# Start offsets of attention and out-projection tiles, the place of the meta keys, and the issue point of a local head's loads

## The chip, the core and the metric

One core of a Trainium2 chip. A core has TensorE (PE, which takes weight loads and matmuls in separate queues, PEld and PE), VectorE (DVE), ScalarE (ACT), GpSimd (POOL) and SyncE (SP, which here issues the DMAs); they run side by side and wait for each other by semaphores. The metric is the device time of one execution in microseconds. Three executions of the kernel before took 2195.36, 2196.57 and 2197.52 us: the median is 2196.57.

## The reference

One layer of an encoder with two groups of heads, run on a prompt of 1024 tokens and a sample of 256, each with 16 meta tokens ahead. All data are float32, the model width is 2048, a head has 128 columns.

```
u = rms_norm(h, norm_w) @ w_in                     # 2048 -> 6656
qa, ka, va, za, qb, kb, vb, zb = split(u)          # a: 8 heads, 2 of keys;  b: 8 heads
ya = global_gqa(rope(norm(qa)), rope(norm(ka)), va) * silu(za)   # every query sees every key
yb = neighbourhood_attention(norm(qb), norm(kb), vb, rpb) * silu(zb)
                                                   # 8 x 16 window on a grid 64 wide, plus the meta keys
y  = concat([ya, yb]) @ w_out                      # 2048 -> 2048
return h + y
```

Heads 0 to 7 are called global here, 8 to 15 local. Only real tokens are returned; the meta tokens take part as 16 more keys of each head.

## The kernel before

A product of two float32 matrices is made in three matmuls: each operand is split into a high part in the type fp32r and the rest (`split`, L59: a CAST on ACT at L61, a subtraction on DVE at L62), and hi×hi, hi×lo and lo×hi are summed in PSUM. A tile is a piece of SBUF that a pool hands out; a pool places its tiles one behind the other, at multiples of 32 bytes in each partition unless the call names `align_bytes`. `ALIGN` is 128 (L35); the tiles of x and of the output weights (`wm`, L917) already name it. A framework draws up the semaphores, and its planner sets the order in which each engine gets its instructions: work is emitted in the order of the program text, weight strips with a higher priority than what stands before them (L185), and the planner fills TensorE's waits with strips.

Three stages follow each other.

*First half* (`chunk1`, L565). 512 columns of tokens: the sample's 256, the prompt's first 240 and 16 of meta tokens. Each strip of 128 columns of w_in is loaded, split and multiplied by all 16 tiles of x (`strips`, L176; the matmuls L210 to L212). Keys, queries, values and gates of the prompt's part go to DRAM: `kd`, `qd` for global heads (two halves, hi and lo), `kfd`, `qfd` for local ones, `vn`, `vmd`, `zd`. The meta keys, the last 16 columns of the strip, are stored ahead of the 240 in `kd` and `kfd`, in a store of their own. The sample's attention is computed here.

*Second half* (`chunk2`, L688). The prompt's other 784 columns, in blocks of 512 and 272. For a global head, `k_first`, `v_tiles`, `q_strip` and `z_strip` make k, v, q and z whole (1024 columns; k has 1040, with the meta keys at columns 0 to 15), and `attend` (L321) runs on four blocks of 256 queries: scores with 8 tiles of keys (L332 to L334), their maxima and sums, exponentials, and probabilities times values (L372 to L374), where `ph` and `pl` are the split probabilities. The 16 meta keys are handled together with their low parts as an operand of 7 × 16 = 112 columns, `km` (`copy_km`, L501; `meta_scores`, L272 and L273), and one matmul with `vm` (L375).

The strips of the local heads (k, q, z, v: 32 in all, `late`) are projected as filling between these blocks and after them; their outputs go to DRAM (`k2d`, `q2d`, `zd`, `vn` by way of transposes L491 and stores L494, L499). The local heads' attention comes from a generator, `local_blocks` (L821): for each head it loads k (`k_load`, L778: `kfd` and `k2d`), v in four windows (`v_windows`), the bias table, q (`q_load`: `qfd` and `q2d`, then a split) and z, and yields after each of four blocks (`attend_strip`, L416: scores L438 on unsplit data, `qfull` and `kfull`, meta scores L272/L273, value products L467 and L470). 28 of its 32 blocks are drawn between the late strips, so that the loads of head h+1 are emitted when the first block of that head is asked for, behind a strip. The pools of k, v, table, q, z and qf have one buffer each, so a load waits until the preceding head has read its tile for the last time.

*Out-projection* (`outproj`, L974). Seven products of half matrices take the place of eight (Winograd's form), in the order 1, 2, 5, 6, 7, 3, 4: five token tiles × two column halves × 24 matmuls each, 70 × 24 = 1680 matmuls (`products`, L935 to L937). The operand loaded into TensorE is `yo` (128 tokens × 8 heads, high and low, from `yd` in DRAM by L884, split at L61/L62), the operand that streams through is `wm` (512 columns, from `ww`). The last local head's four blocks are drawn one after each of the first four products.

All DMAs of this part are issued on SP's queue, in one order; an issue that waits holds all behind it.

Of the kernel before, what the change touches and what calls it, by code (L numbers as in the profile page):

```python
# [20 lines left out]
P = 128  # L21
# [5 lines left out]
NS = 256  # L27
# [27 lines left out]
class Kern:  # L55
# [265 lines left out]
    def attend(self, q, zs, keys, meta, vals, vmeta, ydst):  # L321
# [43 lines left out]
        for j in range(nt):  # L365
            p, i = divmod(j, 2)
            if i == 0:
                ph = self.ph.tile([P, 2, QB], F32R, tag="ph", name="ph")
                pl = self.ph.tile([P, 2, QB], F32R, tag="pl", name="pl")
                self.split(ph[:], pl[:], S[p][:])  # L370
# [45 lines left out]
    def attend_strip(self, q, qf, zs, k, meta, vals, vmeta, tab, w, ydst):  # L416
# [17 lines left out]
        for t in (0, 3, 1, 2):  # L434
            a, e = groups[t]
            dst = part(pa, pb, t)
            o = NMETA + 256 * t + 32 * WIN0[w]
# [63 lines left out]
    def copy_km(self, k):  # L501

        km = self.k.tile([P, 7, NMETA], F32R, tag="km", name="km")
        for i, c, n in ((0, 0, 4), (1, 4, 3)):
            self.nc.scalar.copy(km[:, c:c + n], k[:, i, :].bitcast(F32).unsqueeze(1).to_broadcast([P, n, NMETA]))
        return km[:].rearrange("p c m -> p (c m)")
# [58 lines left out]
    def chunk1(self):  # L565
# [12 lines left out]
        def kb_strip(s, g, wc):  # L578
            kf = self.k.tile([P, T1], F32, tag="k1", name="kcf")

            def evac(ps):
                self.qk_evac(ps[0], 0, T1, wc, None, [], kf[:])
                nc.sync.dma_start(self.kfd[g][:, :NMETA], kf[:, PM:])
                nc.sync.dma_start(self.kfd[g][:, NMETA:], kf[:, NS:PM])
                km = self.k.tile([P, 3, NMETA], F32, tag="km", name="kmf")
                nc.scalar.copy(km[:], kf[:, PM:].unsqueeze(1).to_broadcast([P, 3, NMETA]))
                return kf, km[:].rearrange("p c m -> p (c m)")
# [13 lines left out]
        def k_strip(s, g, wc, rope):  # L601
            kt_ = self.k.tile([P, 2, T1], F32R, tag="k1", name="kc1")

            def evac(ps):
                self.qk_evac(ps[0], 0, T1, wc, (ct, st) if rope else None, [(0, T1, kt_[:, 0, :], kt_[:, 1, :])])
                nc.sync.dma_start(self.kd[g][:, :, :NMETA], kt_[:, :, PM:].bitcast(F32))
                nc.sync.dma_start(self.kd[g][:, :, NMETA:], kt_[:, :, NS:PM].bitcast(F32))
# [80 lines left out]
    def chunk2(self):  # L688
# [10 lines left out]
        K0 = NMETA + C1P  # L699

        def k_first(g):
            k = self.k.tile([P, 2, NMETA + NP], F32R, tag="k1", name="kf")
            nc.sync.dma_start(k[:, :, :K0].bitcast(F32), self.kd[g][:])
            return k, self.copy_km(k[:, :, :NMETA])

        def k_strip(s, g, wc, rope):
            k, km = k_first(g)

            def evac(ps):
                for p, (o, n) in zip(ps, BL):  # L710
                    rp = (ct[:, o:o + n], st[:, o:o + n]) if rope else None
                    self.qk_evac(p, o, n, wc, rp, [(0, n, k[:, 0, K0 + o:K0 + o + n], k[:, 1, K0 + o:K0 + o + n])])
# [10 lines left out]
        def v_tiles(g):  # L723

            h, l = (self.v.tile([P, 8, P], F32R, tag=f"v{i}", name="va") for i in range(2))
# [5 lines left out]
        def v_windows(h):  # L731

            v = []
            for i in range(2):
                t = self.v.tile([P, 8, P], F32, tag=f"v{i}", name="vw")
# [6 lines left out]
        def q_strip(s, h, wc, rope):  # L742
            q = self.q.tile([P, 2, NP], F32R, tag="q", name="q")
# [34 lines left out]
        def k_load(g):  # L778
            k = self.k.tile([P, NMETA + NP], F32, tag="k1", name="kfull")
            nc.sync.dma_start(k[:, :K0], self.kfd[g][:])  # L780
            nc.sync.dma_start(k[:, K0:], self.k2d[g][:])
# [430 lines left out]
```

## Time and profile before

| | |
|---|---|
| median of three executions | 2196.57 us |
| the profiled execution's own time | 2197.35 us |
| its span, first to last instruction | 2195.5 us |
| mean granted TensorE clock | 0.996 |
| busy: PE, PEld, DVE, ACT, POOL | 2166.0, 1879.9, 1650.8, 1125.7, 519.8 us |
| DMA moved | 383.82 MB, mean 175 GB/s |

Times in a profile count from the span's start; 1.85 us of the execution lie outside the span. Matmuls are pipelined: the duration of one (for a projection with 512 columns about 390 ns) is longer than its distance to the next, so a stream's pace is read from the starts. A line such as `L937 PE MATMUL pq<-wm,yo 128*128 128x512 f32 x560 | 223.2, 399 | 0.5 <-DVE yo L62 0.5` gives the line, engine, operation, output and inputs, the loaded operand's shape, the streamed one's, the count, then the busy time in us and the mean of one in ns, then the idle time of the engine just before them and what ended it. PE's busy share in 40 slices is 97% or more in nearly all; the exceptions lie at the start and at 1770 to 1790 us, where the second half ends.

```profile
PE   8999999999999999999999999999999979999999
PEclk9999999999999999999999999999999989999999
```

### The profile page before, as it was taken

To read this page: it belongs to the slowest core of one execution; us is meant where nothing else is said; L and a number is where in the kernel's file an instruction comes from. 1 tells how busy PE (TensorE), PEld (TensorE's weight loads), DVE (VectorE), ACT (ScalarE), POOL (GpSimd) and SP (SyncE) were. 2 spreads that over 40 slices of the span, in tenths; PEclk is the share of its full clock that TensorE was granted. 3 is DMA by queue.
4 is the path that set the end of the run, shared out by engine and by line. 5 is a ranking of instruction groups with operands and counts; after the bars stand their busy time and mean duration, and the time that the engine had idled before them with its cause. 6 is when DMAs were issued, how large, how long until landed. Compare 5 with 4: busy or idle time off the path is not lost.

```text
span 2195.5 us, 34052 instructions
## 1 busy us (share of the span) xinstructions
PE 2166.0 (99%) x11736; PEld 1879.9 (86%) x11736; DVE 1650.8 (75%) x2956; ACT 1125.7 (51%) x2259; POOL 519.8 (24%) x249
## 2 busy tenths in 40 slices
PE   8999999999999999999999999999999979999999
PEld 7888888888878999998999999998989868888887
DVE  8687976778774999995899999777768775545662
ACT  6556544554564667665776665444444444232220
POOL 1232422222212222332223333422322311000000
PEclk9999999999999999999999999999999989999999
DMA  8767898988364334334333336544434363653673
GB/s 296 222 196 228 281 316 297 345 274 264 125 224 143 107 102 116 106 110 143 103 114 110 107 111 197 162 139 139 130 125 133 97 225 113 222 189 124 218 232 108
DMA packets 262173, 383.82 MB, mean 175 GB/s; under 512 B 44880, under 2 KB 113136, under 8 KB 262000
## 3 DMA queue, kind: packets, MB, share of 16 engines
q1 hardware_dynamic: 262000, 381.65, 53.8%
q8 instruction: 92, 1.51, 0.3%
q14 instruction: 81, 0.66, 0.1%
HBM read 281.01 MB, written 100.38 MB: 174 GB/s over the span
## 4 chain that ended last, share of the span: by engine, by line
PE 96%; DMA 2%; DVE 1%; ACT 1%; issue 0%; SPq 0%; DVEq 0%
PE pp L210 21%; PE pp L211 21%; PE pp L212 21%; PE pq L937 6%; PE pq L936 6%; PE pq L935 6%; PE po L470 2%; PE po L372 1%; PE po L374 1%; PE sp L332 1%; PE sp L438 1%; PE po L373 1%; PE sp L334 1%; PE sp L333 1%; DMA ww<-in_w_out 0%; PE tp L491 0%
## 5 line engine op out<-in xcount | busy, mean ns | idle before, releaser
L210 PE MATMUL pp<-x,wh 128*128 128x512 f32 (+1 forms) x2496 | 892.5, 359 | 7.6 <-ACT wh L61 5.9
L211 PE MATMUL pp<-x,wh 128*128 128x512 f32 (+1 forms) x2496 | 889.0, 356 | 0.5 <-DVE x L159 0.4
L212 PE MATMUL pp<-x,wl 128*128 128x512 f32 (+1 forms) x2496 | 888.3, 356 | 0.0
L210 PEld LDWEIGHTS pp<-x,wh 128*128 128x128 f32 x2496 | 469.1, 188 | 72.3 <-ACT wh L61 7.5
L212 PEld LDWEIGHTS pp<-x,wl 128*128 128x128 f32 x2496 | 469.4, 188 | 60.8 <-DVE wl L62 0.7
L211 PEld LDWEIGHTS pp<-x,wh 128*128 128x128 f32 x2496 | 469.8, 188 | 59.7 <-DVE x L159 1.3
L220 POOL PARTITION_ALL_REDUCE m<-ms x78 | 226.0, 2897 | 382.4 <-ACT ms L218 316.3
L62 DVE TENSOR_TENSOR wl<-wr,wh 128x512 fp32r<-128x512 f32 (+1 forms) x290 | 214.5, 742 | 129.6 <-ACT wh L61 106.8
L61 ACT CAST wh<-wr 128x512 fp32r<-128x512 f32 (+1 forms) x290 | 175.1, 608 | 227.4 <-PE pp L211 215.8
L301 POOL PARTITION_ALL_REDUCE tot<-a x80 | 178.3, 2228 | 465.7 <-DVE a L299 461.1
L937 PE MATMUL pq<-wm,yo 128*128 128x512 f32 x560 | 223.2, 399 | 0.5 <-DVE yo L62 0.5
L936 PE MATMUL pq<-wm,yo 128*128 128x512 f32 x560 | 220.8, 394 | 0.0
L935 PE MATMUL pq<-wm,yo 128*128 128x512 f32 x560 | 220.5, 394 | 0.0
L284 POOL PARTITION_ALL_REDUCE ma<-m x80 | 106.3, 1329 | 422.8 <-DVE m L282 422.4
L936 PEld LDWEIGHTS pq<-wm,yo 128*128 128x128 f32 x560 | 105.1, 188 | 26.9
L937 PEld LDWEIGHTS pq<-wm,yo 128*128 128x128 f32 x560 | 105.1, 188 | 25.3 <-DVE yo L62 1.1
L935 PEld LDWEIGHTS pq<-wm,yo 128*128 128x128 f32 x560 | 105.1, 188 | 24.6
L336 ACT COPY S<-sp 128x512 f32<-128x512 f32 x136 | 78.6, 580 | 51.3 <-PE sp L334 40.1
L194 ACT CAST wh<-wr 128x512 fp32r<-128x512 f32 x132 | 81.2, 615 | 40.7 <-PE pp L211 40.7
L62 DVE TENSOR_TENSOR pl<-S,ph 128x512 fp32r<-128x512 f32 x136 | 97.8, 731 | 4.2 <-ACT ph L61 3.9
L61 ACT CAST ph<-S 128x512 fp32r<-128x512 f32 x136 | 83.3, 613 | 34.1 <-PE po L373 33.8
L352 DVE TENSOR_TENSOR S<-S,ma 128x512 f32<-128x512 f32 x136 | 97.2, 772 | 3.9 <-POOL ma L284 3.9
(199 smaller groups left out, 3299.4 us busy)
## 6 DMA issues: line engine op xcount, KB each, us to landing
wr<-in_w_in SPq DMA_DIRECT2D x414, 256.0 KB, 3.4
wld<-wl SPq DMA_DIRECT2D x132, 256.0 KB, 4.3
wl<-wld SPq DMA_DIRECT2D x132, 256.0 KB, 3.2
wq<-in_w_out SPq DMA_DIRECT2D x64, 256.0 KB, 5.1
td<-wq SPq DMA_DIRECT2D x64, 256.0 KB, 4.0
ww<-td SPq DMA_DIRECT2D x64, 256.0 KB, 4.8
yr<-yd SPq DMA_DIRECT2D x30, 512.0 KB, 5.5
ww<-in_w_out SPq DMA_DIRECT2D x48, 256.0 KB, 5.0
```

The source lines that it names most:

```text
L61: self.hi = nc.scalar.copy(hi, full).ins
L62: return nc.vector.tensor_tensor(out=lo, in0=full, in1=hi.bitcast(F32), op=ALU.subtract).ins
L210: nc.tensor.matmul(p[:, :n], wh[:, k, :], xh[:, :n], start=first, stop=False)
L211: nc.tensor.matmul(p[:, :n], wh[:, k, :], xl[:, :n], start=False, stop=False)
L212: nc.tensor.matmul(p[:, :n], wl[:, k, :], xh[:, :n], start=False, stop=last)
L220: nc.gpsimd.partition_all_reduce(m2[:], ms[:], P, RED.add)
L284: nc.gpsimd.partition_all_reduce(ma[:], m1[:], P, RED.max)
L301: nc.gpsimd.partition_all_reduce(tot[:], a1[:], P, RED.add)
L352: nc.vector.tensor_tensor(out=s, in0=s, in1=mb, op=ALU.subtract)
L935: nc.tensor.matmul(ps[:], yh, wh, start=k == 0, stop=False)
L936: nc.tensor.matmul(ps[:], yh, wl, start=False, stop=False)
L937: nc.tensor.matmul(ps[:], yl, wh, start=False, stop=k == 7)
```

## The change

1. `align_bytes=ALIGN` for the tiles of `yo` (both places), of q, k, v (`va`, `vw`) and of the probabilities `ph`, `pl`.
2. The meta keys move from the front of k to its end, and key tile j begins at column 128 j instead of 16 + 128 j. In DRAM, `kd` and `kfd` hold them behind the 240, as they stand in the strip; one store writes both parts. `k_first` and `k_load` load them with one DMA of their own, 16 columns. In `k_first` hi and lo of the meta keys lie behind hi and lo of all keys.
3. `km` tiles get 8 × 16 columns (of which 7 × 16, or 3 × 16, are used).
4. `local_blocks` issues a head's loads right behind the fourth block of the head before, and those of the first at the start of the generator, instead of ahead of the head's own first block.

The number of matmuls and of bytes multiplied stays the same.

```
--- before.py
+++ after.py
@@ -365,8 +365,8 @@
         for j in range(nt):
             p, i = divmod(j, 2)
             if i == 0:
-                ph = self.ph.tile([P, 2, QB], F32R, tag="ph", name="ph")
-                pl = self.ph.tile([P, 2, QB], F32R, tag="pl", name="pl")
+                ph = self.ph.tile([P, 2, QB], F32R, tag="ph", name="ph", align_bytes=ALIGN)
+                pl = self.ph.tile([P, 2, QB], F32R, tag="pl", name="pl", align_bytes=ALIGN)
                 self.split(ph[:], pl[:], S[p][:])
             vh, vl = vals[j]
             nc.tensor.matmul(po[:], vh, ph[:, i, :], start=j == 0, stop=False)
@@ -434,7 +434,7 @@
         for t in (0, 3, 1, 2):
             a, e = groups[t]
             dst = part(pa, pb, t)
-            o = NMETA + 256 * t + 32 * WIN0[w]
+            o = 256 * t + 32 * WIN0[w]
             nc.tensor.matmul(dst, k[:, o:o + P], qfv[:, a:e, :], start=True, stop=True)
             if t == 3:
                 sm = self.meta_scores(pa[:, 256:], meta, qv[:, 0], qv[:, 1], SCALE)
@@ -500,10 +500,10 @@
 
     def copy_km(self, k):
 
-        km = self.k.tile([P, 7, NMETA], F32R, tag="km", name="km")
+        km = self.k.tile([P, 8, NMETA], F32R, tag="km", name="km")[:, :7]
         for i, c, n in ((0, 0, 4), (1, 4, 3)):
             self.nc.scalar.copy(km[:, c:c + n], k[:, i, :].bitcast(F32).unsqueeze(1).to_broadcast([P, n, NMETA]))
-        return km[:].rearrange("p c m -> p (c m)")
+        return km.rearrange("p c m -> p (c m)")
 
@@ -580,11 +580,10 @@
 
             def evac(ps):
                 self.qk_evac(ps[0], 0, T1, wc, None, [], kf[:])
-                nc.sync.dma_start(self.kfd[g][:, :NMETA], kf[:, PM:])
-                nc.sync.dma_start(self.kfd[g][:, NMETA:], kf[:, NS:PM])
-                km = self.k.tile([P, 3, NMETA], F32, tag="km", name="kmf")
-                nc.scalar.copy(km[:], kf[:, PM:].unsqueeze(1).to_broadcast([P, 3, NMETA]))
-                return kf, km[:].rearrange("p c m -> p (c m)")
+                nc.sync.dma_start(self.kfd[g][:], kf[:, NS:])
+                km = self.k.tile([P, 8, NMETA], F32, tag="km", name="kmf")[:, :3]
+                nc.scalar.copy(km, kf[:, PM:].unsqueeze(1).to_broadcast([P, 3, NMETA]))
+                return kf, km.rearrange("p c m -> p (c m)")
             return s, [B0], evac
 
         def qb_strip(s, h, wc):
@@ -603,8 +602,7 @@
 
             def evac(ps):
                 self.qk_evac(ps[0], 0, T1, wc, (ct, st) if rope else None, [(0, T1, kt_[:, 0, :], kt_[:, 1, :])])
-                nc.sync.dma_start(self.kd[g][:, :, :NMETA], kt_[:, :, PM:].bitcast(F32))
-                nc.sync.dma_start(self.kd[g][:, :, NMETA:], kt_[:, :, NS:PM].bitcast(F32))
+                nc.sync.dma_start(self.kd[g][:], kt_[:, :, NS:].bitcast(F32))
                 return kt_, self.copy_km(kt_[:, :, PM:])
             return s, [B0], evac
 
@@ -696,12 +694,12 @@
         self.load_all_x()
         BL = [(0, NB), (NB, T2 - NB)]
 
-        K0 = NMETA + C1P
-
         def k_first(g):
-            k = self.k.tile([P, 2, NMETA + NP], F32R, tag="k1", name="kf")
-            nc.sync.dma_start(k[:, :, :K0].bitcast(F32), self.kd[g][:])
-            return k, self.copy_km(k[:, :, :NMETA])
+            t = self.k.tile([P, 2 * NP + 2 * NMETA], F32R, tag="k1", name="kf", align_bytes=ALIGN)
+            k, m = (x.rearrange("p (i n) -> p i n", i=2) for x in (t[:, :2 * NP], t[:, 2 * NP:]))
+            nc.sync.dma_start(k[:, :, :C1P].bitcast(F32), self.kd[g][:, :, :C1P])
+            nc.sync.dma_start(m.bitcast(F32), self.kd[g][:, :, C1P:])
+            return k, self.copy_km(m)
 
         def k_strip(s, g, wc, rope):
             k, km = k_first(g)
@@ -709,7 +707,7 @@
             def evac(ps):
                 for p, (o, n) in zip(ps, BL):
                     rp = (ct[:, o:o + n], st[:, o:o + n]) if rope else None
-                    self.qk_evac(p, o, n, wc, rp, [(0, n, k[:, 0, K0 + o:K0 + o + n], k[:, 1, K0 + o:K0 + o + n])])
+                    self.qk_evac(p, o, n, wc, rp, [(0, n, k[:, 0, C1P + o:C1P + o + n], k[:, 1, C1P + o:C1P + o + n])])
                 return k, km
             return s, BL, evac
 
@@ -722,7 +720,7 @@
 
         def v_tiles(g):
 
-            h, l = (self.v.tile([P, 8, P], F32R, tag=f"v{i}", name="va") for i in range(2))
+            h, l = (self.v.tile([P, 8, P], F32R, tag=f"v{i}", name="va", align_bytes=ALIGN) for i in range(2))
             nc.sync.dma_start(l[:].bitcast(F32), self.vn[g][:].rearrange("(t p) d -> p t d", p=P))
             nc.scalar.copy(h[:], l[:].bitcast(F32))
             nc.vector.tensor_tensor(out=l[:], in0=l[:].bitcast(F32), in1=h[:].bitcast(F32), op=ALU.subtract)
@@ -732,7 +730,7 @@
 
             v = []
             for i in range(2):
-                t = self.v.tile([P, 8, P], F32, tag=f"v{i}", name="vw")
+                t = self.v.tile([P, 8, P], F32, tag=f"v{i}", name="vw", align_bytes=ALIGN)
                 for j in range(2):
                     o = 32 * WIN0[2 * i + j]
                     nc.sync.dma_start(t[:, 4 * j:4 * j + 4, :], self.vn[2 + h][:].rearrange("(t p) d -> p t d", t=4)[o:o + P])
@@ -740,7 +738,7 @@
             return v, self.load_vm(2 + h)
 
         def q_strip(s, h, wc, rope):
-            q = self.q.tile([P, 2, NP], F32R, tag="q", name="q")
+            q = self.q.tile([P, 2, NP], F32R, tag="q", name="q", align_bytes=ALIGN)
             nc.sync.dma_start(q[:, :, :C1P].bitcast(F32), self.qd[h][:])
 
             def evac(ps):
@@ -776,20 +774,21 @@
             return s, BL, evac
 
         def k_load(g):
-            k = self.k.tile([P, NMETA + NP], F32, tag="k1", name="kfull")
-            nc.sync.dma_start(k[:, :K0], self.kfd[g][:])
-            nc.sync.dma_start(k[:, K0:], self.k2d[g][:])
-            km = self.k.tile([P, 7, NMETA], F32R, tag="km", name="km")
-            full = [k[:, :NMETA].unsqueeze(1).to_broadcast([P, n, NMETA]) for n in (4, 3)]
+            k = self.k.tile([P, NP + NMETA], F32, tag="k1", name="kfull", align_bytes=ALIGN)
+            nc.sync.dma_start(k[:, :C1P], self.kfd[g][:, :C1P])
+            nc.sync.dma_start(k[:, C1P:NP], self.k2d[g][:])
+            nc.sync.dma_start(k[:, NP:], self.kfd[g][:, C1P:])
+            km = self.k.tile([P, 8, NMETA], F32R, tag="km", name="km")[:, :7]
+            full = [k[:, NP:].unsqueeze(1).to_broadcast([P, n, NMETA]) for n in (4, 3)]
             nc.scalar.copy(km[:, :4], full[0])
             nc.vector.tensor_tensor(out=km[:, 4:], in0=full[1], in1=km[:, :3].bitcast(F32), op=ALU.subtract)
-            return k, km[:].rearrange("p c m -> p (c m)")
+            return k, km.rearrange("p c m -> p (c m)")
 
         def q_load(h):
             qf = self.qf.tile([P, NP], F32, tag="qf", name="qfull")
             nc.sync.dma_start(qf[:, :C1P], self.qfd[h][:])
             nc.sync.dma_start(qf[:, C1P:], self.q2d[h][:])
-            q = self.q.tile([P, 2, NP], F32R, tag="q", name="q")
+            q = self.q.tile([P, 2, NP], F32R, tag="q", name="q", align_bytes=ALIGN)
             self.split(q[:, 0, :], q[:, 1, :], qf[:])
             return q, qf
 
@@ -811,7 +810,7 @@
                                   self.yd[1][:, b // 2:NP // P:2, h - 8, 64 * (b % 2):64 * (b % 2) + 64])
                 return
             c = slice(QB * b, QB * b + QB)
-            keys = [(k[:, 0, o:o + P], k[:, 1, o:o + P]) for o in range(NMETA, NMETA + NP, P)]
+            keys = [(k[:, 0, o:o + P], k[:, 1, o:o + P]) for o in range(0, NP, P)]
             self.attend(q[:, :, c], z[:, c], keys, km, v, vm[:], self.yd[0][:, 2 * b:2 * b + 2, h, :])
 
         def run(h, q, z, k, v, tab):
@@ -819,11 +818,17 @@
                 run_block(h, b, q, z, k, v, tab)
 
         def local_blocks():
-            for h in range(NH):
+            def load(h):
                 k, v = k_load(2 + h), v_windows(h)
                 tab, q, z = self.bias_table(h, "bt", (3, 384)), q_load(8 + h), z_load(8 + h)
+                return q, z, k, v, tab
+
+            tiles = load(0)
+            for h in range(NH):
                 for b in range(4):
-                    run_block(8 + h, b, q, z, k, v, tab)
+                    run_block(8 + h, b, *tiles)
+                    if b == 3 and h + 1 < NH:
+                        tiles = load(h + 1)
                     yield
 
         pr = self.project
@@ -880,7 +885,7 @@
             return r[:]
 
         if p in (1, 2, 4):
-            r = self.yo.tile([P, 2, 8, P], F32R, tag="yo", name="yo")
+            r = self.yo.tile([P, 2, 8, P], F32R, tag="yo", name="yo", align_bytes=ALIGN)
             self.nc.sync.dma_start(r[:, 1].bitcast(F32), self.yd[p > 1][:, NT * (p == 4) + t])
             return r
         return [half(*x) for x in {7: [(0, 0), (0, 1)], 5: [(0, 1), (1, 1)], 6: [(0, 0)], 3: [(1, 0)]}[p]]
@@ -897,7 +902,7 @@
             v = self.ysum[t][:]
             a, b, op = {5: (r[0], r[-1], ALU.add), 6: (v, r[0], ALU.subtract), 3: (r[0], v, ALU.subtract)}[p]
             nc.vector.tensor_tensor(out=v, in0=a, in1=b, op=op)
-        o = self.yo.tile([P, 2, 8, P], F32R, tag="yo", name="yo")
+        o = self.yo.tile([P, 2, 8, P], F32R, tag="yo", name="yo", align_bytes=ALIGN)
         self.split(o[:, 0], o[:, 1], v)
         return o
 
```

69 lines of the change are left out of this document (37 added, 32 removed).

## The prediction

> **What bounds the kernel now.** I read the page's first part and its chain first, then the windows at the places where the order of work changes, then TensorE's timeline row by row.
>
> ```profile
> span 2195.5 us, 34052 instructions
> PE 2166.0 (99%) x11736; PEld 1879.9 (86%) x11736; DVE 1650.8 (75%) x2956; ACT 1125.7 (51%) x2259; POOL 519.8 (24%) x249
> PE 96%; DMA 2%; DVE 1%; ACT 1%; issue 0%; SPq 0%; DVEq 0%
> ```
>
> TensorE is busy 2166.0 of 2195.5 us and holds 96% of the chain that ended last; weight loads run beside it. So two things can move the time: the distance between two matmul starts in a stream, and the holes, which hold 29.5 us in all. The windows (stretch, its length, then PE, PEld, DVE, ACT, POOL, granted clock, DMA share, GB/s) show where a hole is, and where none can be filled:
>
> ```profile
> 1300.00:1400.00 100.00, 100.00 (x630) 91.45 (x629) 90.43 (x188) 57.37 (x126) 38.51 (x21) 1.00 0.57 171
> 1770.00:1780.00 10.00, 1.03 (x5) 0.41 (x3) 7.92 (x17) 6.01 (x14) 0.00 (x0) 0.61 0.94 318
> 1780.00:1790.00 10.00, 5.02 (x20) 4.56 (x21) 7.87 (x16) 5.46 (x11) 2.19 (x2) 0.54 1.05 405
> ```
>
> At 1300 to 1400, where the first local head begins, TensorE has no gap. At 1770 to 1790, where the last local head and the out-projection begin, it works 6 of 20 us, DMA is saturated, and the granted clock drops to 0.54.
>
> The matmul's own duration overlaps its neighbours', so I take the step from start to start: first and last row of an unbroken stream, divided by the matmuls between.
>
> ```profile
> 449.25 0.39 PE L210 MATMUL pp<-x,wh 128*128 128x512 f32 x1
> ...
> 459.92 0.39 PE L212 MATMUL pp<-x,wl 128*128 128x512 f32 x1
> 1835.11 0.53 PE L935 MATMUL pq<-wm,yo 128*128 128x512 f32 x1
> ...
> 2191.32 0.40 PE L937 MATMUL pq<-wm,yo 128*128 128x512 f32 x1
> ```
>
> The first stream is a projection, 48 matmuls: 10.67 us / 47 = 227.0 ns. The second is the out-projection. The next row is its matmuls alone (tile pq) to 2191.00; two more start behind it, so 1527 in all, and 356.21 us / 1526 = 233.4 ns. It is busy 355.89 of 356 us at a clock of 1.00, so these 6.4 ns are not waits.
>
> ```profile
> 1835.00:2191.00 356.00, 355.89 (x1525) 286.33 (x1526) 39.80 (x59) 8.20 (x14) 1.00 0.54 182
> ```
>
> Both shapes are 128 columns loaded, 512 moved, same type. The program as built puts x, wh, wl and wm at multiples of 128 bytes, and yo, the loaded operand of L935 to L937, at 32 bytes past one. This offset is the one difference I find that the diff removes.
>
> **The change part by part.** *Alignment of yo.* It removes no instruction; TensorE issues the same matmuls.
>
> ```profile
> L937 PE MATMUL pq<-wm,yo 128*128 128x512 f32 x560 | 223.2, 399 | 0.5 <-DVE yo L62 0.5
> L936 PE MATMUL pq<-wm,yo 128*128 128x512 f32 x560 | 220.8, 394 | 0.0
> L935 PE MATMUL pq<-wm,yo 128*128 128x512 f32 x560 | 220.5, 394 | 0.0
> ```
>
> 1680 matmuls × 6.4 ns = 10.75 us. Nothing else paces them (DVE is at 39.80 of 356 us on this tile, DMA at 0.54), so the gain would arrive in full. The bounds are 0 (the step has another cause) and 10.75 (the projection's step is reached); I take 10.75, the projection being the only other stream of this shape.
>
> *Alignment of q, k, v and probabilities for the global heads.* Before, all of these start 64 bytes past a multiple of 128.
>
> ```profile
> 646.75 0.28 PE L210 MATMUL pp<-x,wh 128*128 128x272 f32 x1
> ...
> 649.62 0.29 PE L212 MATMUL pp<-x,wl 128*128 128x272 f32 x1
> 772.90 0.28 PE L333 MATMUL sp<-q,kf 128*128 128x256 f32 x1
> ...
> 775.16 0.28 PE L334 MATMUL sp<-q,kf 128*128 128x256 f32 x1
> L332 PE MATMUL sp<-q,kf 128*128 128x256 f32 x256 | 70.9, 282 | 0.0
> L334 PE MATMUL sp<-q,kf 128*128 128x256 f32 x256 | 71.4, 280 | 0.0
> L372 PE MATMUL po<-ph,va 128*128 128x256 f32 x256 | 72.2, 282 | 0.0
> L374 PE MATMUL po<-pl,va 128*128 128x256 f32 x256 | 72.0, 281 | 0.0
> L375 PE MATMUL po<-Pm,vm 128*128 128x256 f32 x40 | 11.6, 290 | 0.3 <-DVE Pm L294 0.2
> ```
>
> Attention steps: 2.26 us / 19 = 118.9 ns at 256 moved columns. No aligned stream has 256 columns, but the aligned 272 gives 2.87 / 23 = 124.8 ns, and (227.0 − 124.8) / 240 = 0.426 ns for each column, so an aligned 256 should take 124.8 − 16 × 0.426 = 118.0 ns. At most 0.9 to 1.0 ns can be had: 64 past costs far less than 32 past, if the offset is the cause at all. L332 to L334 and L372 to L374, each 256 times, are 1536 matmuls; bounds 0 and 1.0 ns, I take 0.6, so −0.9 us (0 to −1.5).
>
> *Meta keys.* The meta tiles km get eight columns of 16 instead of seven in the pool; in the built program ten of the second half's lie 96 past a multiple of 128, where before they were at 0.
>
> ```profile
> L272 PE MATMUL sm_ps<-q,km 128*112 128x256 f32 x32 | 9.0, 282 | 0.0
> L273 PE MATMUL sm_ps<-q,km 128*112 128x256 f32 x32 | 9.0, 281 | 0.0
> ```
>
> Two lines with two forms of 32 (the local heads' read alike), 128 matmuls. If 96 costs what 32 does, 6.4 ns each: +0.8 us; the other bound is 0. I take +0.8.
>
> *DMA.* Ten stores of meta keys go into their neighbours; each of the ten k loads has one more DMA of 64 bytes a row. An issue takes 0.33 to 0.42 us of SP's queue (rows below); ten fewer and ten more cancel. All but the last head's ride under a full TensorE; uncovered, a load would be late by one landing, 3.4 to 7.6 us (the yo loads' lowest and highest).
>
> *Loads of a local head behind the preceding head's blocks.* As built, the order on PE, ACT, DVE and SP is that of before except for single swaps, outside two places. At 1325 to 1420 the first local head's matmuls are shuffled; TensorE is busy 100.00 of 100 there, so a shuffle costs nothing so long as the weight strips beside it are ready: 0, with ±2.2 us as its bounds (the 2.20 us wait in the first row below, the nearest one for a local head's operand). If that cover fails, the next thing late is the strip's weight cast, and TensorE with it.
>
> The second place is the last head. Rows of PE, ACT and SP (what stands in brackets is idle time before the row, and who ended it):
>
> ```profile
> 1772.33 0.90 PE L491 MATMUL tp<-ident,vt 128*128 128x128 f32 x3 [2.20 <-ACT vl L493]
> ...
> 1784.75 2.47 PE L438 MATMUL sp<-qfull,kfull 128*128 128x128 f32 x8 [11.52 <-DMA ww<-in_w_out]
> ...
> 1791.11 0.53 PE L935 MATMUL pq<-wm,yo 128*128 128x512 f32 x1
> 1769.72 0.33 SPq L780 DMA_DIRECT2D kfull<-kfd  x1
> ...
> 1771.53 0.42 SPq L781 DMA_DIRECT2D kfull<-k2d  x1
> ...
> 1775.80 0.55 SPq L494 DMA_DIRECT2D vn<-vl  x1
> 1777.47 0.32 SPq L499 DMA_DIRECT2D vn<-vl  x1
> ...
> 1779.16 0.33 SPq L791 DMA_DIRECT2D qfull<-q2d  x1
> 1779.84 3.82 SPq L912 DMA_DIRECT2D ww<-in_w_out  x6
> 1783.75 1.10 SPq L884 DMA_DIRECT2D yo<-yd  x2
> 1785.17 1.00 SPq L738 DMA_DIRECT2D vw<-vn  x2
> 1789.68 1.05 ACT L61 CAST yo<-yo 128x1024 fp32r<-128x1024 f32 x1 [1.50 <-DMA yo<-yd]
> ```
>
> The 11.52 us hole ends when the last head's q lands: its second half is issued only at 1779.16, behind weights of the out-projection, and L438 starts 5.6 us later (the row's label names a weight transfer that had landed before). The out-projection starts at 1791.11, 1.43 us after ACT began to cast the first yo; that yo was issued at 1783.75.
>
> In the new order the k and q loads go ahead of the weights, and two vw loads ahead of the first yo. From the first k load to the first yo, SP issues 19 transfers instead of 23, 4.93 MB instead of 6.24 MB by their shapes. The missing 1.31 MB at 405 GB/s are 3.2 us by which the first yo comes sooner; following each issue to its landing gave me 3 to 4.5 us. I take −3.5. Bounds: q could be issued with k, at 1771.53 instead of 1779.16, −7.6 us at most. On the other side, vw reads the vn stores: issued by 1777.47 and landing up to 7.6 us later, they hold vw until 1785.1, yo leaves at 1786.1, lands by 1793.7, and the first L935 comes 1.43 us behind, 1795.1: +4.0. Behind SP's wait for them stand the yo loads and seven weights of the next pass. The cover against this is that scores of two more blocks now come before, which need only k and q.
>
> The sum, against the profiled execution's own 2197.35 us (span 2195.5 and 1.85 around it): −10.75 − 3.5 − 0.9 + 0.8 = −14.35, so 2183.0. That execution lies 0.78 above the median 2196.57, so on the median's scale **2182.2 us**.
>
> **The rivals.** *(a) The offset does not set the step.* The 6.4 ns would then belong to something else in L935 to L937 (wm, the moved operand, is written over while the stream runs, say). For it: no pair of rows differs in offset alone, and attention at 64 past shows almost no price. Against it: the step is constant over 356 us with nothing waiting. Only the transition's 3.5 remain: 2197.35 − 3.5 − 0.78 = 2193.1. The Trainium skill ("TensorE: Matmul & The Clock Gate", "Wait — 56ns, not 53.3ns?") speaks for this rival: a warm stream steps by columns ÷ 2.4 GHz plus a fixed 2.5 ns, 215.7 ns at 512, with no term for an address. The trace disagrees with the figure twice (227.0 and 233.4 at clock 1.00), so that rule lacks a term here, whichever it is.
>
> *(b) The transition gives nothing,* since the vw loads wait for the vn stores as worked out above: the sum without its 3.5 is 2182.2 + 3.5 = 2185.7, and with the +4.0, 2189.7.
>
> *(c) Slower: operands that all start at the same multiple collide.* The one attention group whose operands both lie at 0 already, L375, has a mean of 290 ns against 280 to 282 for those at 64. If that is a collision and not the 48 rows of its operand, the 1536 aligned matmuls pay 8 ns each, +12.3 us, and the out-projection, aligned like the projection, is no better for it: 2197.35 + 12.3 − 3.5 − 0.78 = 2205.4. It decides from (3.5 + 4.4) / 1536 = 5.1 ns on. Against it: the projection, all at 0, has the shorter step.
>
> **How the numbers follow.** Main forecast 0.60, (a) 0.17, (b) 0.13, (c) 0.10. A measurement of this kernel can tell 0.2% from no change, 4.4 us: 2192.2 to 2201.0. Main and (b) are faster, and of (a) about 0.05 (when the transition gives over 4.4); (a)'s other 0.12 is no change; (c) is slower. The range goes from 2175, where every term lies at its favourable bound (2196.57 − 10.75 − 7.6 − 1.5 = 2176.7, and the first head's 2.2), to 2195, which takes in (a) with a smaller gain at the transition and leaves out (c). The likeliest case's own range is 2176 to 2189.
>
> **What would show each step.** The out-projection's stream should step at 227 ± 1 ns instead of 233.4, its 1527 matmuls taking 10 us less; if it stays at 233.4, the main term is wrong and (a) holds. Attention steps should be 118.0 to 118.9; above 124, (c). L272 and L273 should read some 6 ns longer. The hole before L438 (11.52) should be shorter, q2d issued before the run of weights, and the first L935 3 to 4.5 us earlier against the last transposes; if the cast of yo comes later than 17.4 us behind them, (b). Between 1300 and 1400 TensorE should stay at 100.

## The result: 3.0 us where 14.4 were forecast, and the profile after

The changed kernel takes 2193.63 us in the median (2190.31 to 2196.47, 18 runs), the kernel before 2196.64 (2195.36 to 2201.06, 18 runs). The ratio is 0.9985, 95% interval 0.9979 to 0.9992: faster, by 3.0 us. The forecast was 2182.2. The time is close to that of rival (a), 2193.1; how much of this is luck is told further down.

The page of the changed kernel, its first part and its chain:

```profile
span 2191.8 us, 34025 instructions
PE 2165.2 (99%) x11736; PEld 1881.7 (86%) x11736; DVE 1646.2 (75%) x2956; ACT 1124.4 (51%) x2259; POOL 518.2 (24%) x249
PE 94%; DVE 2%; DMA 2%; ACT 1%; issue 1%; SPq 0%; POOL 0%; DVEq 0%; ACTq 0%; POOLq 0%
```

TensorE is as busy as before, with as many matmuls. The span is 3.7 us shorter. Where these went is seen by laying starts of the same matmul side by side, at the ends of three stretches: 0.4 us up to the last local head, 2.0 us from there to 1845 us, 1.2 us in the rest of the out-projection.

The out-projection alone (windows of tile pq: stretch, length, PE, PEld, DVE, ACT, clock, DMA share, GB/s), first before, then after. Dividing 310 us by the count in brackets gives the step within 0.4 ns; the steps in the text are taken from first start to last.

```profile
1840.00:2150.00 310.00, 310.00 (x1330) 249.32 (x1329) 34.99 (x52) 7.61 (x13) 1.00 0.58 195
```

```profile
1840.00:2150.00 310.00, 310.00 (x1334) 251.05 (x1333) 35.64 (x53) 7.59 (x13) 1.00 0.59 197
```

1330 and 1334 matmuls in the same 310 us: the step went from 233.3 to 232.4 ns, not to 227. Four more matmuls in 310 us is what aligning yo to 128 bytes bought.

The pattern of single steps says more than the mean. Before, they repeat every three matmuls: 231, 232, 237 ns, 700 ns for three. After, every seven: 232, 231, 232, 228, 230, 233, 241. The projection repeats 227, 227, 226. All of these are patterns without any wait, at a granted clock of 1.00.

The transition to the out-projection, TensorE's rows of after (in brackets the idle time and its releaser):

```profile
1771.90 0.55 PE L491 MATMUL tp<-ident,vt 128*128 128x128 f32 x3 [2.19 <-ACT vl L493]
1776.49 2.47 PE L438 MATMUL sp<-qfull,kfull 128*128 128x128 f32 x8 [4.05 <-DMA qfull<-q2d]
...
1781.87 0.68 PE L438 MATMUL sp<-qfull,kfull 128*128 128x128 f32 x4 [2.48 <-DVE S L443]
...
1786.73 0.58 PE L467 MATMUL po<-Pm,vm 128*128 128x256 f32 x1 [3.29 <-DVE Pm L294]
...
1788.99 0.88 PE L940 MATMUL pq<-wm,yo 128*128 128x512 f32 x1
```

and of SP's queue:

```profile
1771.10 0.43 SPq L790 DMA_DIRECT2D qfull<-q2d  x1
...
1779.53 0.93 SPq L736 DMA_DIRECT2D vw<-vn  x2
1780.55 0.45 SPq L889 DMA_DIRECT2D yo<-yd  x1
```

q's second half leaves at 1771.10 instead of 1779.16, as foreseen, and the hole ahead of the last head's first scores falls from 11.52 to 4.05 us. But two new holes stand behind it, 2.48 and 3.29. In DVE's rows one sees what stands ahead of the work that they wait for:

```profile
1777.50 1.23 DVE L62 TENSOR_TENSOR q<-qfull,q 128x1024 fp32r<-128x1024 f32 x1 [2.36 <-ACT q L61]
1778.64 0.68 DVE L62 TENSOR_TENSOR wm<-ww,wm 128x512 fp32r<-128x512 f32 x1
1779.25 0.28 DVE L455 TENSOR_TENSOR m<-m,S 128x128 f32<-128x128 f32 x1
...
1786.26 0.42 DVE L294 TENSOR_TENSOR Pm<-Sm,Pm 16x256 fp32r<-16x256 f32 x1
```

The same two steps of that softmax in the kernel before:

```profile
1779.34 0.28 DVE L455 TENSOR_TENSOR m<-m,S 128x128 f32<-128x128 f32 x1
...
1787.52 0.41 DVE L294 TENSOR_TENSOR Pm<-Sm,Pm 16x256 fp32r<-16x256 f32 x1
```

The split of the last head's q now stands in DVE's order ahead of the softmax of the preceding head's fourth block, and it waits 2.36 us for ACT's cast, which waits for q's DMA. L455 of that softmax starts at 1779.25, against 1779.34 before, and L294, which its value products wait for, at 1786.26 against 1787.52. So q comes 8 us sooner and the softmax only 1.3 us, and its value products stand ahead of the first product of the out-projection on TensorE. The split of q is not the only holder: splits of weights stand in DVE's order ahead of L455 and behind it, and on ACT four casts of weights, 1781.57 to 1784.03, stand ahead of this softmax's exponentials, which start at 1784.31.

### The profile page after: what moved, and what is told of

It reads as the page before. It is cut to its first block, busy times and chain, and to the rows that moved or that the text cites. A ratio compares the mean times of both kernels' runs of the same rounds, so it can differ in the third digit from the quotient of the medians.

```text
span 2191.8 us, 34025 instructions
## 1 busy us (share of the span) xinstructions
PE 2165.2 (99%) x11736; PEld 1881.7 (86%) x11736; DVE 1646.2 (75%) x2956; ACT 1124.4 (51%) x2259; POOL 518.2 (24%) x249
## 4 chain that ended last, share of the span: by engine, by line
PE 94%; DVE 2%; DMA 2%; ACT 1%; issue 1%; SPq 0%; POOL 0%; DVEq 0%; ACTq 0%; POOLq 0%
PE pp L210 21%; PE pp L211 21%; PE pp L212 21%; PE pq L942 6%; PE pq L941 6%; PE pq L940 6%; PE po L470 2%; PE sp L438 1%; PE sp L333 1%; PE sp L334 1%; PE sp L332 1%; PE po L374 1%; PE po L372 1%; PE po L373 1%; DMA ww<-in_w_out 0%
## 5 line engine op out<-in xcount | busy, mean ns | idle before, releaser
L210 PE MATMUL pp<-x,wh 128*128 128x512 f32 (+1 forms) x2496 | 892.4, 359 | 7.3 <-ACT wh L61 5.5
L211 PE MATMUL pp<-x,wh 128*128 128x512 f32 (+1 forms) x2496 | 888.6, 356 | 0.4 <-DVE x L159 0.4
L212 PE MATMUL pp<-x,wl 128*128 128x512 f32 (+1 forms) x2496 | 888.7, 356 | 0.0
L210 PEld LDWEIGHTS pp<-x,wh 128*128 128x128 f32 x2496 | 469.1, 188 | 71.6 <-ACT wh L61 7.0
L212 PEld LDWEIGHTS pp<-x,wl 128*128 128x128 f32 x2496 | 469.6, 188 | 60.9 <-DVE wl L62 0.7
L211 PEld LDWEIGHTS pp<-x,wh 128*128 128x128 f32 x2496 | 469.9, 188 | 59.9 <-DVE x L159 1.3
```

What stands on the lines that cost most here:

```text
L210: nc.tensor.matmul(p[:, :n], wh[:, k, :], xh[:, :n], start=first, stop=False)
L211: nc.tensor.matmul(p[:, :n], wh[:, k, :], xl[:, :n], start=False, stop=False)
L212: nc.tensor.matmul(p[:, :n], wl[:, k, :], xh[:, :n], start=False, stop=last)
```

## The experiments

All times of the kernel before that they are compared with lie between 2196.8 and 2197.5 us (medians of the runs on the same chip). "Step" is the mean distance between starts in the out-projection's unbroken stream. Both operands' start addresses are known from the built program; they are given modulo 256 bytes.

**Undo the alignment of yo in the changed kernel** (both places):

```
-            r = self.yo.tile([P, 2, 8, P], F32R, tag="yo", name="yo", align_bytes=ALIGN)
+            r = self.yo.tile([P, 2, 8, P], F32R, tag="yo", name="yo")
```

> The changed kernel with yo back at 32 past a multiple of 128; wm stays at 128 past a multiple of 256, as in both kernels. Theory O (the offset of yo sets part of the step of the out-projection): its step goes back from the 232.4 ns of the changed kernel to the 233.4 of the kernel before, 1526 x 1.0 = 1.5 us slower than the changed kernel, 2195.1. Theory W (only the start of wm counts, and the 1.0 ns between the two traces is which pattern the stream happened to fall into): the step may be either, anything from 2193.6 to 2195.1, and does not follow yo in all of the runs to come.

Measured: 2195.08 us (2193.42 to 2196.24, 11 runs; ratio 0.9987, 0.9978 to 0.9996), step 233.3 ns in a pattern of three.

**The kernel before with yo alone at multiples of 128** (`align_bytes=ALIGN` in those two lines):

> The kernel before with yo alone at multiples of 128; all else as before. Theory O: a step of 232.4 ns instead of 233.4, 1.5 us off, 2195.1, and the transition at 1770 to 1790 us as in the kernel before. Theory of the prediction (the full 6.4 ns): 227 ns and 2185.9; the changed kernel's trace already speaks against it. Theory W: the step stays within 232 to 234 whatever yo does.

Measured: 2195.56 us (11 runs; ratio 0.9992, 0.9983 to 1.0000), step 232.4 in the pattern of seven. So the step follows yo in all four kernels: 32 past a multiple of 128 gives 233.3, 0 gives 232.4. It is an effect of 1 ns, worth about 1.5 us, which the times alone, with intervals that reach to 0.9996 and 1.0000, would hardly show. (A run further down has both values at one and the same distance, so that the offset is the cause of this 1 ns is likely, not shown.) The other 5.6 ns must have another reason.

What differs still? The start offsets, taken modulo 128, are 0 for wm, x, wh and wl alike. Taken modulo 256, x, wh and wl are at 0 and wm is at 128. The next two kernels move it.

**wm at multiples of 256** (yo goes to 128 past one, since its pool lies below):

```
-        w = self.wm.tile([P, 2, FB], F32R, tag="wm", name="wm", align_bytes=ALIGN)
+        w = self.wm.tile([P, 2, FB], F32R, tag="wm", name="wm", align_bytes=256)
```

> The changed kernel with the tiles of wm at multiples of 256 instead of 128; by this yo comes to lie at 128 past a multiple of 256. In both kernels so far wm, the streamed operand, lies at 128 past a multiple of 256 and the projection's x at a multiple of 256. Theory W (the streamed operand must start at a multiple of 256): the step falls to the projection's 226.7 to 227.0 ns, 1680 x 5.6 = 9.4 us faster than the changed kernel, 2184. Theory B (both operands must start at multiples of 256): no change or little, 2193. Theory S (the step belongs to the form of the stream, not to addresses): 2193.6.

**wm and yo at multiples of 256** (the same edit for the two lines of yo as well):

> The changed kernel with both wm and yo at multiples of 256. Theory W: 226.7 to 227.0 ns, 2184, the same as with wm alone. Theory B: 226.7 to 227.0 ns and 2184 here only. Theory S (not the addresses): 232 to 234 ns, 2193.6.

The rows of tile pq, first with wm alone, then with both:

```profile
1840.00:2150.00 310.00, 310.00 (x1331) 249.38 (x1330) 35.20 (x53) 7.59 (x13) 1.00 0.59 197
```

```profile
1840.00:2150.00 310.00, 310.00 (x1368) 256.51 (x1367) 36.30 (x54) 7.61 (x13) 1.00 0.60 202
```

With wm alone: 1331, a step of 233.3 (now in a pattern of two, 238 and 229), 2194.0 us (11 runs; ratio 0.9986, 0.9977 to 0.9994). So it is not the streamed operand's own boundary. With both: 1368 matmuls in 310 us, a step of 226.7 in the projection's own pattern of 227, 227, 226, and 2183.78 us (2183.25 to 2185.05, 5 runs; ratio 0.994, 0.9926 to 0.9954). Against the run with yo at 32 past, 2195.08, these are 11.3 us: the forecast's 10.75 are there, one factor of two in the alignment away.

Two theories are left: each operand must start at a multiple of 256 (B), or the two must only start at the same place modulo 256 (R).

**Both at 128 past a multiple of 256**, by a filler of 32 floats ahead of yo in its tile, wm as in the changed kernel:

```
-            r = self.yo.tile([P, 2, 8, P], F32R, tag="yo", name="yo", align_bytes=ALIGN)
+            r = self.yo.tile([P, 32 + 2048], F32R, tag="yo", name="yo", align_bytes=256)[:, 32:].rearrange("p (i k n) -> p i k n", i=2, k=8)
... (the tile `o` of the second place alike)
```

> The changed kernel with yo moved to 128 past a multiple of 256 (by a filler in its tile), so that yo and wm both lie at 128. Theory B (each of the two must start at a multiple of 256): the step stays at 232 to 234 ns, 2193 to 2196. Theory R (only the distance between the two operands counts, which is 0 here as in the run with both at 256): 226.7 ns and 2184.

```profile
1840.00:2150.00 310.00, 310.00 (x1368) 256.51 (x1368) 36.32 (x54) 7.61 (x13) 1.00 0.60 201
```

1368 again, 2183.78 us (4 runs; ratio 0.9939, 0.9923 to 0.9954). B falls: neither operand starts at a multiple of 256 here. What the two fast kernels share is the distance, 0. The writing of wm goes on beside the stream as before (in these 310 us 96 instructions of ACT and 96 of DVE on that tile, here and in the kernel before), so it is not what the 6.6 ns were paid for.

**The reverse, on the projection**: in the kernel before, 128 bytes more in the filler at the right end of SBUF move x to 128 past a multiple of 256, while wh and wl, at the left end, stay. (wm and yo move together; their distance stays 160.)

```
-                self.pad.tile([P, 24], F32, name="pad")
+                self.pad.tile([P, 56], F32, name="pad")
```

> The kernel before with everything on the right side of SBUF 128 bytes lower: x comes to lie at 128 past a multiple of 256 (wh and wl stay at multiples of 256), wm at a multiple of 256, yo at 160 past one. Theory B: the projection with 512 columns, 226.7 ns so far, steps at 232 to 234 ns as the out-projection does; of its 3456 matmuls some 2965 lie in unbroken streams, so 16 to 20 us slower for these alone, and the 496-column ones lose about as much each (1536 of them): 2205 to 2225. Theory S (the out-projection's stream is slow or fast for reasons of its own): the projection stays at 226.7, 2196 to 2198.

The same stream as that at 449.25 to 459.92 before:

```profile
453.85 0.40 PE L210 MATMUL pp<-x,wh 128*128 128x512 f32 x1
...
464.82 0.39 PE L212 MATMUL pp<-x,wl 128*128 128x512 f32 x1
```

10.97 us / 47 = 233.4 ns instead of 227.0. The kernel takes 2213.96 us (ratio 1.0077, 1.0063 to 1.0090), 16.7 us more, from one filler and no change of work. The out-projection keeps its 233.3. So the step belongs to the addresses, in both stages, and not to the form of the out-projection. In the first half of this same kernel the long streams of 512 columns step at 232.3 to 232.5 ns (64 steps from 130.55 to 145.43 us, for one), in the second half at 233.3 to 233.4, with the same addresses modulo 512: at a distance of 128 a stream can fall into either.

**Attention too.** In the changed kernel, at multiples of 128, q, one half of v and `ph` lie at 128 modulo 256, the keys at 0. Here all of them are at 0 for the global heads of the second half, placed by sizes instead of `align_bytes`, on top of wm and yo at multiples of 256. Three of the edits:

```
-        km = self.k.tile([P, 8, NMETA], F32R, tag="km", name="km")[:, :7]
+        km = self.k.tile([P, 10, NMETA], F32R, tag="km", name="km")[:, :7]
-        rope = self.tab.tile([P, 2, T2], F32, tag="bt", name="rope2")
+        rope = self.tab.tile([P, 2, T2 + 16], F32, tag="bt", name="rope2")
...
-        q = self.q.tile([P, 2, NP], F32R, tag="q", name="q", align_bytes=ALIGN)
+        q = self.q.tile([P, 2, NP], F32R, tag="q", name="q")
...
```

> The kernel with wm and yo at multiples of 256, and besides q, k, v and the probabilities of the second half at multiples of 256 (in the changed kernel, at multiples of 128, q, one half of v and ph lie at 128 past a multiple of 256). Theory B carried to 256 columns with the same 5.6 ns: 1536 x 5.6 = 8.6 us, 2175. Against it the slope of the two aligned streams, 220.0 ns at 496 columns and 226.7 at 512, gives 0.417 ns for each column and 226.7 - 256 x 0.417 = 120.0 ns at 256, while the mixed 256-column stream already has 118.3: then nothing is gained, 2183.8 to 2186.

The first unbroken stream of 256 columns in the changed kernel, then here; the third row of each is the start of a later stream, as a landmark:

```profile
772.97 0.28 PE L333 MATMUL sp<-q,kf 128*128 128x256 f32 x1
...
775.22 0.29 PE L334 MATMUL sp<-q,kf 128*128 128x256 f32 x1
...
1259.20 0.28 PE L333 MATMUL sp<-q,kf 128*128 128x256 f32 x1
```

```profile
771.93 0.28 PE L333 MATMUL sp<-q,kf 128*128 128x256 f32 x1
...
774.20 0.28 PE L334 MATMUL sp<-q,kf 128*128 128x256 f32 x1
...
1259.29 0.28 PE L333 MATMUL sp<-q,kf 128*128 128x256 f32 x1
```

The same 19 steps take 2.27 us, 119.5 ns, against 2.25, 118.4; and between the two landmarks 487.36 us against 486.23, 1.1 us more (with wm and yo alone at 256 it is 486.3). The whole takes 2186.09 us (2183.24 to 2188.09, 5 runs), against 2183.78 (2183.25 to 2185.05) without this edit, ranges that overlap; the landmarks are the surer reading. At 256 columns, distance 0 is no gain; it costs about 1 ns. That 119.5 lies near the 120.0 of the expectation's slope proves little, since the 220.0 at 496 columns that the slope starts from is only one of two values, as shown below.

**Early loads alone**: the kernel before with the new `local_blocks`.

> The kernel before with the new place of the local heads' loads alone. By the two traces the transition at 1770 to 1790 us is 1.7 us shorter in the changed kernel, so 2197.5 - 1.7 = 2195.8 if that comes from the place of the loads; if it comes from the meta keys' own DMA or the layout instead, 2197.5. The hole before the first scores of the last head should fall from 11.52 to 4 to 5 us, with new waits of 2 to 3 us behind it on DVE's results.

Measured: 2195.59 us (2194.7 to 2197.02, 11 runs; ratio 0.9993, 0.9984 to 1.0002), which can't be told from no change. The hole is 3.13 us, and the new waits are there:

```profile
1775.70 2.47 PE L438 MATMUL sp<-qfull,kfull 128*128 128x128 f32 x8 [3.13 <-DMA qfull<-q2d]
...
1781.68 1.19 PE L438 MATMUL sp<-qfull,kfull 128*128 128x128 f32 x4 [3.08 <-DVE S L443]
...
1786.85 0.58 PE L467 MATMUL po<-Pm,vm 128*128 128x256 f32 x1 [2.27 <-DVE Pm L294]
```

With the 2.20 ahead of the last transposes, its holes sum to 10.7 us, against 14.4 before (2.20 + 11.52 + 0.23 + 0.49). Of these 3.7 us only 0.6 are left at 1845 us. Where the others went shows in windows of six microseconds, at 1790 to 1796, first before, then here:

```profile
1790.00:1796.00 6.00, 5.51 (x29) 4.40 (x28) 5.82 (x12) 3.95 (x7) 2.56 (x2) 1.00 1.10 358
```

```profile
1790.00:1796.00 6.00, 6.00 (x24) 5.11 (x24) 5.76 (x11) 1.94 (x4) 1.10 (x1) 0.74 1.08 385
```

Here TensorE is busy all six, and starts 24 matmuls instead of 29: the granted clock is 0.74 instead of 1.00. In this run the work put into the holes ran at a clock of about 0.5, and the full clock came back later. From the last strip to 1845 us the trace with yo put back to 32 gains 1.0 us on the kernel before, and those of the changed kernel itself, of wm at 256 and of the distances 32 and 64 below gain 1.8 to 2.2: by the trace, the transition is worth 0.6 to 2.2 us.

**The two alignments alone, on the kernel before** (wm and yo at multiples of 256, nothing else of the change):

> The kernel before with yo and wm at multiples of 256 and nothing else of the change: attention tiles, meta keys and the place of the loads stay. Theory R (only the distance between the two operands of the out-projection, taken modulo 256, counts, 0 here): its step is 226.7 ns, 1680 x 6.7 = 11.2 us off the kernel before, 2186. If the early loads were needed for that, or the transition grew, less.

Measured: 2186.82 us (2185.89 to 2187.07, 5 runs; ratio 0.9954, 0.9941 to 0.9968), step 226.7 ns. 10.0 of the 11.2 us arrived.

**Other distances** (the filler of the run with both at 128, of 8, 16 and 48 floats, with wm at multiples of 256):

> The changed kernel with wm at multiples of 256 and yo 32 bytes past one, distance 32. Theory R1 (any distance but 0 costs the whole 6 ns): 232 to 234 ns, 2193 to 2196. Theory R2 (the cost grows with the distance): below 230 ns, 2184 to 2190.

> The same with yo 64 bytes past a multiple of 256, distance 64. Theory R1: 232 to 234 ns, 2193 to 2196. Theory R2: between that of distance 32 and the 232.4 to 233.3 of distance 128. Theory R3 (what matters is whether both fall into the same part of 128 bytes): 226.7 ns here and at 32, 2184.

> The same with yo 192 bytes past a multiple of 256; the distance is 192, or 64 to the other side. Theory R1: 232 to 234 ns, 2193 to 2196. Theory R2: as at 64, if the distance counts alike to both sides. Theory R3: 232 to 234 ns.

Measured: 2195.52, 2195.78 and 2187.70 us. The rows of tile pq for 32 and for 192:

```profile
1840.00:2150.00 310.00, 310.00 (x1330) 249.63 (x1329) 34.93 (x52) 7.59 (x13) 1.00 0.58 197
```

```profile
1840.00:2150.00 310.00, 310.00 (x1356) 254.36 (x1355) 36.35 (x54) 7.60 (x13) 1.00 0.60 199
```

All that was measured for 512 columns in long unbroken streams, by the distance from the streamed operand's start to the loaded one's, modulo 256:

| distance | where | step, ns |
|---|---|---|
| 0 | projection; both at 0; both at 128; on the kernel before | 226.7 to 227.7 |
| 32 | out-projection | 233.3 |
| 64 | out-projection | 233.3 |
| 128 | changed kernel and before with yo alone, wm at 128 | 232.4 |
| 128 | wm at 0, yo at 128 | 233.3 |
| 128 | projection with x at 128 | 232.3 to 233.4 |
| 160 | kernel before | 233.3 |
| 192 | out-projection | 228.9 |

R1, that any distance but 0 costs the whole, holds at four of five distances; 192 costs a third of it, and neither R2 nor R3 foresaw that.

Other shapes keep this from being a rule for all. At 496 columns two streams of the kernel before, both at distance 0, differ by as much as a distance does:

```profile
32.12 0.38 PE L210 MATMUL pp<-x,wh 128*128 128x496 f32 x1
...
52.14 0.38 PE L211 MATMUL pp<-x,wh 128*128 128x496 f32 x1
```

```profile
173.03 0.39 PE L212 MATMUL pp<-x,wl 128*128 128x496 f32 x1
...
194.24 0.39 PE L211 MATMUL pp<-x,wh 128*128 128x496 f32 x1
```

20.02 us / 91 = 220.0 ns, and 21.21 / 95 = 223.3. With x at 128 six of the seven long streams of this shape step at 226.4 to 226.5, one at 223.3. At 272 columns no price is seen: L211 alone is at distance 128 in the kernel before, L210 and L212 instead of it in the run with x at 128, and unbroken streams of 12 matmuls and more step at 125.3 and 125.2 ns in the mean.

## Why the prediction was wrong

**The step that failed is the alignment of yo**: "1680 matmuls × 6.4 ns = 10.75 us", with the reason "This offset is the one difference I find that the diff removes." The 6.4 ns were real, and were the price of addresses. But the offsets had been listed modulo 128, the multiple that the diff names, and there x, wh, wl and wm look alike. Modulo 256 wm stands apart, and at 512 columns it is the distance between the two operands that decides between 227 and up to 233 ns. The diff changed that distance from 160 to 128: from one slow value to another, 1.0 ns apart. So what the diff removes is 1680 × 0.9 ns = 1.5 us of these 10.75. Nothing in one profile showed the modulus; that no pair of rows differed in offset alone, which the text on rival (a) says, was the warning, and taking the full 10.75 was the choice against it. Of the bounds 0 and 10.75, these 1.5 us lie near the lower.

**Rival (a)** came nearest. It was right that the offset which the diff removes does not set the step (1.0 of the 6.4 ns), and that the rest belongs to something else in L935 to L937. Its example of that, wm written over while the stream runs, was wrong, and it did not think of wm's address: the runs with both at 256, both at 128, and x moved to 128 show that addresses set the step. That its 2193.1 meets 2193.63 is in part luck: it takes 3.5 us from the transition, which gave 0.6 to 2.2, and nothing from yo, which gave about 1.5. The rule of the Trainium skill that spoke for it ("TensorE: Matmul & The Clock Gate", "Wait — 56ns, not 53.3ns?": columns ÷ 2.4 GHz plus a fixed 2.5 ns, 215.7 ns at 512) has no term for an address. The traces disagree: 226.7 at distance 0, 233.3 at 32. (The streams of that section's example are bf16, these are fp32r.) The skill's lines of 16 bytes ("SBUF — State Buffer", "Specifications (TRN2)") don't account for it either, since 32 and 64 are whole lines and cost 6.6 ns.

**Attention**, −0.9 us: in the first unbroken stream the step fell from 118.9 to 118.4, about as worked out. But only six such streams of 20 matmuls are among the 1536; the others lie between strips. From the first landmark to the last the kernel before takes 1259.41 − 772.90 = 486.51 us, by

```profile
1259.41 0.28 PE L333 MATMUL sp<-q,kf 128*128 128x256 f32 x1
```

and the changed kernel 486.23: 0.3 us. The term's sign was right and its size a third. Its reason, that aligned is better, doesn't hold: in the run with attention at distance 0 these tiles start at multiples of 128 too, and the step is 119.5. Two readings of the prediction were off here. The keys' low half, which L334 loads, already began at a multiple of 128 in the kernel before (it lies 1040 × 4 = 4160 bytes behind the high half), so one of the six lines had less to gain. And the 272 columns that served as the aligned stream have one line in three at a distance of 128.

**Meta keys**, +0.8: not there. From its start to the next one, L272 of tile `sm_ps` takes 119.7 ns in the mean and L273 117.3, against 119.1 and 117.8 before. Their durations, which the prediction wanted to read, don't rise either, though a duration says little of a step: 281 and 280 ns, 282 and 281 before.

```profile
L272 PE MATMUL sm_ps<-q,km 128*112 128x256 f32 x32 | 9.0, 281 | 0.0
L273 PE MATMUL sm_ps<-q,km 128*112 128x256 f32 x32 | 9.0, 280 | 0.0
```

**The first local head**, 0: right; TensorE stays busy 100.00 of 100 us at 1300 to 1400, and the 0.4 us by which its starts lead there are still 0.4 at the last strips. The DMA's 0 is not contradicted by any run.

**The transition**, −3.5: the mechanism came as described (q ahead of the weights, the hole from 11.52 to 4.05), and 2.0 us arrived in the trace of after, 0.6 to 2.2 over the traces, within the bounds. By the sign that the prediction had set, the first product against the last transposes, it is 1.7 us (1788.99 − 1771.90 = 17.1, against 18.8), not 3 to 4.5. What was not seen is that the split of q would stand ahead of the preceding block's softmax on DVE, and, in the run with the early loads alone, that work moved into holes ran at half the clock. Rival (b)'s condition, the cast of yo more than 17.4 us behind the last transposes, was not met: it comes 14.4 us behind them (1786.27), and the first product no longer waits for yo at all, but for that softmax.

**Rival (c)**, a collision at 256 columns, shows at most as about 1 ns at distance 0, not 8, and the changed kernel brings only two of the six lines there, L373 and L374.

All but the alignment of yo was forecast at −3.5 − 0.9 + 0.8 = −3.6 us. Two pairs of medians measure these parts: 2197.51 to 2195.08 without any edit of yo, −2.4, and 2186.82 to 2183.78 with the out-projection already at distance 0, −3.0 (−3.7 with each taken against the kernel before on its own chip). That part of the sum was near, but its terms were not: 0.6 to 2.2, 0.3 and 0 us are what the traces give for them, so the nearness is partly luck. The fastest kernel measured is the changed one with wm and yo at the same place modulo 256, 2183.78 us.

## What to carry to other kernels

Compare start addresses of the two operands of a matmul with each other, modulo 256, not each with a boundary; here 512-column streams of fp32r step at 226.7 ns when they agree and at up to 233.4 when they don't, while streams of 256 and 272 columns gained nothing by it. In this kernel, which TensorE bounds, 128 bytes of filler cost 16.7 us and 256 for 128 in three `align_bytes` saved about 10, so after any change of layout read the step from first and last start of an unbroken stream, and put it beside the fastest stream of the same shape. When a load is moved forward, follow its consumers in the order of every engine: here part of the wait moved from the DMA's queue into DVE's order, in front of older work.

## What had not been expected of the hardware

Steps without any wait settle into repeating patterns: 227, 227, 226 at distance 0; 231, 232, 237 at 160; 238 and 229, or a cycle of seven, at 128. A stream that is broken into finds its pattern again: in the run with both at 256, two steps of 343 and 339 ns at 2079.6 us are followed by five of 229 to 235, and then 227, 227, 226 is back. What makes the distance count, why 192 costs 2.2 ns where 32 to 160 cost 5.7 to 6.6, and what decides between two values at one distance, no run here shows.

The granted clock in the transition is as much a term as the holes: at 1790 to 1796 us it was 1.00 in the kernel before and 0.74 with the early loads alone. The Trainium skill ("TensorE: Matmul & The Clock Gate", "What's actually happening") has the array go to half speed after an idle window of about 3.4 us and come back after a busy one; the windows agree with the half, 0.50 at 1778 to 1784 and at 1784 to 1790 in that run:

```profile
1778.00:1784.00 6.00, 2.92 (x12) 2.62 (x11) 5.62 (x13) 3.71 (x8) 1.36 (x1) 0.50 1.06 398
1784.00:1790.00 6.00, 3.73 (x15) 3.23 (x14) 5.08 (x13) 3.96 (x7) 1.79 (x1) 0.50 1.06 393
```

TensorE was at work for about half of these twelve microseconds, in pieces, and the clock stayed at 0.50. The share of work alone does not decide it: with as much work in the first of these windows, 2.97 us against 2.92, the changed kernel has 0.78.

```profile
1778.00:1784.00 6.00, 2.97 (x16) 2.34 (x14) 5.97 (x13) 3.86 (x7) 1.06 (x1) 0.78 1.06 383
```

That the pieces were too short for a busy window fits, but no run here shows it.
